# Batch norm on one core: the context closed after the first issues, parameter rows on ScalarE's queue, the first tile in one transfer

## The chip, the cores and the metric

The kernel runs on one core of a Trainium2 chip; the other cores are idle. The metric is the device time of one execution in microseconds, the median over the runs shown. Lower is better.

## The reference

The input `x` is float32 of shape (32, 256, 128, 128), 537 MB. Each of the 256 channels has its own gamma, beta, running mean and running variance:

```python
mean = running_mean.reshape(1, -1, 1, 1)
var = running_var.reshape(1, -1, 1, 1)
return gamma * (x - mean) / np.sqrt(var + 1e-5) + beta
```

For each channel this is one scale, gamma / sqrt(var + eps), and one shift, beta - mean * scale, applied to every element. All of `x` is read once and an output of the same size is written once.

## The kernel before

**Tiles.** A tile is 128 channels of one image: 128 partitions by 128 * 128 = 16384 float32, 8.39 MB. There are 32 * 2 = 64 of them (`NT`), taken in `order`: first all images' lower 128 channels, then the upper ones. Three buffers t0, t1, t2 (`NBUF`) hold tiles in SBUF; tile i lies in buffer i % 3 and is overwritten in place by its result.

**Engines.** SyncE issues the loads, on DMA queue q1. VectorE computes the first 14336 columns (`VCOLS`) of a tile in two instructions, 2560 (`STEP`) and 11776 wide (L162, L163, both through L133). ScalarE computes the last 2048 columns (L144) and issues the store (L157), on DMA queue q10. In the last tile VectorE does 9216 columns (`VLAST`) and ScalarE 7168.

**Order.** Everything stands in one `tc.tile_critical()` block with waits written by hand, so no scheduler orders it. `loaded[s]`, `stored[s]` count the transfers of a buffer (16 for each finished one), `vdone` VectorE's parts, `adone` ScalarE's.

- Load i, from the fourth on, waits until the store of tile i-3 has left its buffer and until VectorE has done the first part of tile i-1 (L104 to L107). So one load is in flight at a time.
- VectorE's first part of tile i waits until tile i has landed.
- ScalarE's part of tile i waits until VectorE has finished the tile and until the store of tile i-1 has landed (L165 to L169). So one store is in flight at a time.

**Parameters.** The four parameter vectors are loaded as rows: each is broadcast into 16 partitions of `rows`, 1 KB in each (L94). VectorE transposes 32x32 blocks (L111) and copies them (L116), so that a channel's values come to its partition. ScalarE takes the square root (L118); VectorE makes the reciprocal, the scale and the shift (L125 to L128). The helper `step` chains these on the semaphore `vec`.

**The beginning.** SyncE issues, in this order: the left half of tile 0 (L91, semaphore `early`), the four rows (L94, the first waits for the memset of `rows` at L92), the right half of tile 0 (L98), then tiles 1 and 2 whole (L105). VectorE does the left half of tile 0 when `early` and the parameters are there, the rest (6144 columns) when the right half has landed (L159, L160).

**The end.** SyncE waits for the last store of each buffer (L175). Then the tile context is closed: every engine goes through barriers, and GpSimd clears the context's semaphores. The buffers come from pools of the context, after a filler of 936 columns (`PAD`).

Of the kernel before, what the change touches and what calls it, by code (L numbers as in the profile page):

```python
# [8 lines left out]
NBUF = 3  # L9
PAD = 936  # L10


STEP = 2560
VCOLS = 14336
VLAST = 9216


@with_exitstack
def kernel(
    ctx: ExitStack,  # L20
    tc: tile.TileContext,
    x: bass.AP,
    gamma: bass.AP,
    beta: bass.AP,
    running_mean: bass.AP,
    running_var: bass.AP,
    out: bass.AP,
):
    nc = tc.nc
    eps = 1e-5  # L30
    f32 = mybir.dt.float32

    N, C, H, W = x.shape
    P = nc.NUM_PARTITIONS
    assert C % P == 0
    NCB = C // P
    HW = H * W
    NT = N * NCB
    B = 32
    NQ = P // B  # L40
    NE = 16
    NPAR = 4

    xr = x.rearrange("n (cb p) h w -> (n cb) p (h w)", p=P)
    outr = out.rearrange("n (cb p) h w -> (n cb) p (h w)", p=P)

    params = ctx.enter_context(tc.tile_pool(name="params", bufs=1))
    data = ctx.enter_context(tc.tile_pool(name="data", bufs=1))
    params.tile([P, PAD], f32, name="pad", tag="pad")
    bufs = [data.tile([P, HW], f32, name=f"t{s}", tag=f"t{s}") for s in range(NBUF)]  # L50
    rows = params.tile([B, NPAR * C], f32, name="rows", tag="rows")
    turned = params.tile([B, NPAR * C], f32, name="turned", tag="turned")
    par = params.tile([P, NPAR, NCB], f32, name="par", tag="par")
    eps_t = params.tile([P, 1], f32, name="eps_t", tag="eps")
    std_t = params.tile([P, NCB], f32, name="std_t", tag="std")
    rstd_t = params.tile([P, NCB], f32, name="rstd_t", tag="rstd")
    scale_t = params.tile([P, NCB], f32, name="scale_t", tag="scale")
    ms_t = params.tile([P, NCB], f32, name="ms_t", tag="ms")
    shift_t = params.tile([P, NCB], f32, name="shift_t", tag="shift")

    loaded = [tc.alloc_semaphore(f"loaded{s}") for s in range(NBUF)]
    stored = [tc.alloc_semaphore(f"stored{s}") for s in range(NBUF)]
    early = tc.alloc_semaphore("early")
    vdone = tc.alloc_semaphore("vdone")
    adone = tc.alloc_semaphore("adone")
    fetched = tc.alloc_semaphore("fetched")
    vec = tc.alloc_semaphore("vec")
    act = tc.alloc_semaphore("act")  # L70

    with tc.tile_critical():  # L72
        count = [0]

        def step(inst, sem=None, value=None):

            if sem is not None:
                inst._wait_ge(sem, value)
            elif count[0]:
                inst._wait_ge(vec, count[0])  # L80
            inst.then_inc(vec, 1)
            count[0] += 1
            return count[0]

        left, right = slice(0, HW // 2), slice(HW // 2, HW)
        last = NT - 1
        order = [n * NCB + cb for cb in range(NCB) for n in range(N)]

        nc.sync.dma_start(out=bufs[0][:, left], in_=xr[order[0]][:, left]).then_inc(early, 16)  # L91
        zeroed = step(nc.vector.memset(rows[:], 0.0))  # L92
        for r, ap in enumerate((running_var, gamma, beta, running_mean)):
            inst = nc.sync.dma_start(out=rows[0:NE, r * C : (r + 1) * C], in_=ap.partition_broadcast(NE))  # L94
            if r == 0:
                inst._wait_ge(vec, zeroed)
            inst.then_inc(fetched, 16)
        nc.sync.dma_start(out=bufs[0][:, right], in_=xr[order[0]][:, right]).then_inc(loaded[0], 16)  # L98
        for i in range(1, NT):
            s, turn = i % NBUF, i // NBUF  # L100


            if turn:
                nc.sync.wait_ge(stored[s], 16 * turn)  # L104
            inst = nc.sync.dma_start(out=bufs[s][:], in_=xr[order[i]]).then_inc(loaded[s], 16)  # L105
            if turn:
                inst._wait_ge(vdone, 2 * (i - 1) + 1)  # L107


        step(nc.vector.memset(eps_t[:], eps))  # L110
        step(nc.vector.transpose(out=turned[:], in_=rows[:]), fetched, 16 * NPAR)  # L111

        blocks = turned.rearrange("p (rc q b) -> p rc q b", q=NQ, b=B)
        flat = par.rearrange("p r cb -> p (r cb)")
        for q in range(NQ):
            placed = step(nc.vector.tensor_copy(out=flat[q * B : (q + 1) * B], in_=blocks[:, :, q, 0]))  # L116
        var_t, gamma_t, beta_t, mean_t = (par[:, r] for r in range(NPAR))
        nc.scalar.activation(  # L118
            out=std_t[:],
            in_=var_t,  # L120
            func=mybir.ActivationFunctionType.Sqrt,
            bias=eps_t[:],
            scale=1.0,
        )._wait_ge(vec, placed).then_inc(act, 1)
        step(nc.vector.reciprocal(out=rstd_t[:], in_=std_t[:]), act, 1)  # L125
        step(nc.vector.tensor_mul(out=scale_t[:], in0=gamma_t, in1=rstd_t[:]))  # L126
        step(nc.vector.tensor_mul(out=ms_t[:], in0=mean_t, in1=scale_t[:]))  # L127
        ready = step(nc.vector.tensor_sub(out=shift_t[:], in0=beta_t, in1=ms_t[:]))  # L128
        nc.vector.wait_ge(vec, ready)

        def vector_part(i, first, end):
            t, cb = bufs[i % NBUF], order[i] % NCB
            return nc.vector.tensor_scalar(  # L133
                out=t[:, first:end],
                in0=t[:, first:end],
                scalar1=scale_t[:, cb : cb + 1],
                scalar2=shift_t[:, cb : cb + 1],
                op0=mybir.AluOpType.mult,
                op1=mybir.AluOpType.add,
            ).then_inc(vdone, 1)  # L140

        def scalar_part(i, first):
            t, cb = bufs[i % NBUF], order[i] % NCB
            return nc.scalar.activation(  # L144
                out=t[:, first:],
                in_=t[:, first:],
                func=mybir.ActivationFunctionType.Identity,
                bias=shift_t[:, cb : cb + 1],
                scale=scale_t[:, cb : cb + 1],
            ).then_inc(adone, 1)  # L150

        def landed(i):
            return loaded[i % NBUF], 16 * (i // NBUF + 1)

        def store(i):
            s = i % NBUF
            nc.scalar.dma_start(out=outr[order[i]], in_=bufs[s][:])._wait_ge(adone, i + 1).then_inc(stored[s], 16)  # L157

        vector_part(0, 0, HW // 2)._wait_ge(early, 16)  # L159
        vector_part(0, HW // 2, VCOLS)._wait_ge(*landed(0))  # L160
        for i in range(1, NT):
            vector_part(i, 0, STEP)._wait_ge(*landed(i))  # L162
            vector_part(i, STEP, VLAST if i == last else VCOLS)  # L163
        for i in range(last):
            nc.scalar.wait_ge(vdone, 2 * (i + 1))  # L165
            inst = scalar_part(i, VCOLS)
            if i:
                inst._wait_ge(stored[(i - 1) % NBUF], 16 * ((i - 1) // NBUF + 1))
            store(i)  # L169
        scalar_part(last, VLAST)._wait_ge(*landed(last))  # L170
        nc.scalar.wait_ge(vdone, 2 * NT)
        store(last)

        for s in range(NBUF):
            nc.sync.wait_ge(stored[s], 16 * ((NT - s + NBUF - 1) // NBUF))  # L175


# [28 lines left out]
```

## Time and profile before

| | |
|---|---|
| runs | 2482.06, 2484.93 and 2484.79 us |
| median | 2484.79 us |
| span of the profiled execution (first to last instruction) | 2481.7 us |
| VectorE busy | 508.8 us |
| ScalarE busy | 140.0 us |
| bytes moved, mean rate over the span | 1073.85 MB, 433 GB/s |
| first load issued | 0.95 us after the first instruction |
| tile 0 landed (right half) | 23.61 us |
| first store issued | 29.27 us |
| first load that waits for a buffer (load 3) issued | 89.36 us |
| last store landed | 2480.4 us |

The page gives no time of the profiled execution other than its span. Idle time of an engine is listed with what ended it. The two largest items show what the compute engines wait for:

```profile
L133 DVE TENSOR_SCALAR t<-t,scale_t,shift_t 128x11776 f32<-128x11776 f32 (+2 forms) x128 | 505.3, 3989 | 1929.1 <-DMA t<-in_x_dram 1929.0
L144 ACT ACTIVATE t<-t,shift_t,scale_t 128x2048 f32<-128x2048 f32 x64 | 138.4, 2163 | 2297.8 <-DMA out_dram<-t 2275.0
```

The columns are: line, engine, operation, output and inputs, shape, count; busy us and mean ns of one; idle us of the engine just before them and what ended most of it. VectorE (DVE) waits for loads, ScalarE (ACT) for stores. The DMA queues are listed with packets, bytes and the time of their packets as a share of 16 engines' span:

```profile
q1 hardware_dynamic: 9488, 536.94, 50.1%
q10 hardware_dynamic: 9216, 536.88, 49.9%
```

q1 holds what SyncE issued, q10 what ScalarE issued. A tile is 128 data packets of 64 KB, one for each partition, and 16 packets of 4 bytes that count up its semaphore, one for each DMA engine. Behind the page lies a record for each packet with its queue, start, duration and size; where the text speaks of packet records, it means these.

### The profile page before, as it was taken

What the parts mean: (1) busy time and instruction counts of PE and PEld (TensorE: products, weight loads), DVE (VectorE), ACT (ScalarE), POOL (GpSimd) and SP (SyncE); (2) the same over time, 40 slices, a digit from 0 to 9 for tenths busy, and PEclk for the clock granted to TensorE, in tenths of its full rate; (3) what the DMA queues carried; (4) which work ended last, traced back from release to release, by engine and by line L of the source; (5) the groups of instructions that cost most, each with busy time, mean ns of one, the idle gap of its engine ahead of it and who ended that gap; (6) DMA issues with size and microseconds to landing.
All of it is one profiled execution on the core that took longest, in us unless ns stands there. A gap on an engine that the chain in (4) does not pass through costs nothing.

```text
span 2481.7 us, 516 instructions
## 1 busy us (share of the span) xinstructions
DVE 508.8 (21%) x139; ACT 140.0 (6%) x66; POOL 0.2 (0%) x4
## 2 busy tenths in 40 slices
DVE  2122121221212212122121221212212122121120
ACT  0000000000000000000000000000000000000001
POOL 0000000000000000000000000000000000000000
DMA  9999999999999999999999999999999999999999
GB/s 418 427 437 436 428 435 438 429 436 436 431 434 436 435 430 436 429 436 435 430 436 435 434 431 431 434 436 435 431 435 437 429 435 437 429 436 436 433 433 408
DMA packets 18708, 1073.85 MB, mean 433 GB/s; under 512 B 2128, under 2 KB 2192, under 8 KB 2192
## 3 DMA queue, kind: packets, MB, share of 16 engines
q1 hardware_dynamic: 9488, 536.94, 50.1%
q10 hardware_dynamic: 9216, 536.88, 49.9%
q14 instruction: 4, 0.03, 0.0%
HBM read 536.94 MB, written 536.87 MB: 433 GB/s over the span
## 4 chain that ended last, share of the span: by engine, by line
DMA 92%; DVE 4%; another core or an unknown queue 2%; ACT 0%; issue 0%; SPq 0%; DVEq 0%
DMA t<-in_x_dram 92%; DVE t L133 4%; ACT t L144 0%; SPq L94 0%; DVE rows L92 0%; DVE eps_t L110 0%; DVEq L201 0%; SPq L72 0%
## 5 line engine op out<-in xcount | busy, mean ns | idle before, releaser
L133 DVE TENSOR_SCALAR t<-t,scale_t,shift_t 128x11776 f32<-128x11776 f32 (+2 forms) x128 | 505.3, 3989 | 1929.1 <-DMA t<-in_x_dram 1929.0
L144 ACT ACTIVATE t<-t,shift_t,scale_t 128x2048 f32<-128x2048 f32 x64 | 138.4, 2163 | 2297.8 <-DMA out_dram<-t 2275.0
L111 DVE STREAM_TRANSPOSE turned<-rows 32x1024 f32<-32x1024 f32 x1 | 1.2, 1232 | 12.1 <-DMA rows<-in_running_mean_dram 12.1
L118 ACT ACT_TABLE_LOAD x1 | 1.3, 1283 | 0.9 <-SPq L72 0.9
L92 DVE MEMSET rows<- 32x1024 f32 x1 | 0.9, 912 | 1.2 <-SPq L72 1.2
L118 ACT ACTIVATE std_t<-par,eps_t 128x2 f32<-128x2 f32 x1 | 0.3, 297 | 14.3 <-DVE par L116 14.3
L116 DVE COPY par<-turned 32x8 f32<-32x8 f32 x4 | 0.6, 161 | 0.1
L125 DVE RECIPROCAL rstd_t<-std_t 128x2 f32<-128x2 f32 x1 | 0.2, 166 | 0.4 <-ACT std_t L118 0.4
L127 DVE TENSOR_TENSOR ms_t<-par,scale_t 128x2 f32<-128x2 f32 x1 | 0.2, 161 | 0.0
L128 DVE TENSOR_TENSOR shift_t<-par,ms_t 128x2 f32<-128x2 f32 x1 | 0.2, 161 | 0.0
L126 DVE TENSOR_TENSOR scale_t<-par,rstd_t 128x2 f32<-128x2 f32 x1 | 0.2, 160 | 0.0
L190 POOL MEMSET const-uint8-127<- 128x1 uint8 x1 | 0.1, 102 | 0.0
L190 POOL MEMSET const-bfloat16-1.0<- 128x1 bf16 x1 | 0.1, 101 | 0.0
L190 POOL MEMSET const-float32-0.0<- 128x1 f32 x1 | 0.1, 99 | 0.2 <-issue 0.2
L190 POOL MEMSET const-float32-1.0<- 128x1 f32 x1 | 0.1, 99 | 0.0
L110 DVE MEMSET eps_t<- 128x1 f32 x1 | 0.1, 59 | 0.1
## 6 DMA issues: line engine op xcount, KB each, us to landing
t<-in_x_dram SPq DMA_DIRECT2D x2, 4096.0 KB, 16.2
out_dram<-t ACTq DMA_DIRECT2D x64, 36.5
t<-in_x_dram SPq DMA_DIRECT2D x63, 37.0
rows<-in_running_var_dram SPq DMA_DIRECT2D x1, 16.0 KB, 11.3
rows<-in_gamma_dram SPq DMA_DIRECT2D x1, 16.0 KB, 11.2
rows<-in_beta_dram SPq DMA_DIRECT2D x1, 16.0 KB, 11.0
rows<-in_running_mean_dram SPq DMA_DIRECT2D x1, 16.0 KB, 10.9
```

Of the source, the lines that this page charges most:

```text
L92: zeroed = step(nc.vector.memset(rows[:], 0.0))
L110: step(nc.vector.memset(eps_t[:], eps))
L111: step(nc.vector.transpose(out=turned[:], in_=rows[:]), fetched, 16 * NPAR)
L116: placed = step(nc.vector.tensor_copy(out=flat[q * B : (q + 1) * B], in_=blocks[:, :, q, 0]))
L118: nc.scalar.activation(out=std_t[:], in_=var_t, func=mybir.ActivationFunctionType.Sqrt, bias=eps_t[:], scale=1.0,)._wait_ge(vec, placed).t ...
L125: step(nc.vector.reciprocal(out=rstd_t[:], in_=std_t[:]), act, 1)
L126: step(nc.vector.tensor_mul(out=scale_t[:], in0=gamma_t, in1=rstd_t[:]))
L127: step(nc.vector.tensor_mul(out=ms_t[:], in0=mean_t, in1=scale_t[:]))
L128: ready = step(nc.vector.tensor_sub(out=shift_t[:], in0=beta_t, in1=ms_t[:]))
L133: return nc.vector.tensor_scalar(out=t[:, first:end], in0=t[:, first:end], scalar1=scale_t[:, cb : cb + 1], scalar2=shift_t[:, cb : cb + 1 ...
L144: return nc.scalar.activation(out=t[:, first:], in_=t[:, first:], func=mybir.ActivationFunctionType.Identity, bias=shift_t[:, cb : cb + 1] ...
L190: nc = _bacc.Bacc("TRN2", target_bir_lowering=False, num_devices=1)
```

## The change

1. The tile context is closed early. Only the memset of `rows`, the loads of tiles 0, 1 and 2 and the four row transfers stay inside; then come `tc.close()` and `tc.compile()`, and all that follows is issued plainly behind the context's closing barriers. The waits by hand are the same. Buffers and semaphores no longer come from the context, and SyncE clears the semaphores itself after the last store.
2. The four row transfers are issued by ScalarE in place of SyncE, and so go on queue q10.
3. Tile 0 is loaded in one transfer of 16384 columns. The semaphore `early` is gone, and VectorE treats tile 0 as every other tile: 2560 and 11776 columns after the whole has landed.

The filler and the sizes of the buffers stay. The core of the diff:

```diff
-    params = ctx.enter_context(tc.tile_pool(name="params", bufs=1))
-    data = ctx.enter_context(tc.tile_pool(name="data", bufs=1))
-    params.tile([P, PAD], f32, name="pad", tag="pad")
-    bufs = [data.tile([P, HW], f32, name=f"t{s}", tag=f"t{s}") for s in range(NBUF)]
+    def tile_of(name, *shape):
+        return nc.alloc_sbuf_tensor(name, list(shape), f32)
...
+    tile_of("pad", P, PAD)
+    bufs = [tile_of(f"t{s}", P, HW) for s in range(NBUF)]
...
+    sems = {name: nc.alloc_semaphore(name) for name in names}
...
     with tc.tile_critical():
-        nc.sync.dma_start(out=bufs[0][:, left], in_=xr[order[0]][:, left]).then_inc(early, 16)
+        nc.sync.dma_start(out=bufs[0][:], in_=xr[order[0]]).then_inc(loaded[0], 16)
         zeroed = step(nc.vector.memset(rows[:], 0.0))
         for r, ap in enumerate((running_var, gamma, beta, running_mean)):
-            inst = nc.sync.dma_start(out=rows[0:NE, r * C : (r + 1) * C], in_=ap.partition_broadcast(NE))
+            inst = nc.scalar.dma_start(out=rows[0:NE, r * C : (r + 1) * C], in_=ap.partition_broadcast(NE))
             if r == 0:
                 inst._wait_ge(vec, zeroed)
             inst.then_inc(fetched, 16)
-        nc.sync.dma_start(out=bufs[0][:, right], in_=xr[order[0]][:, right]).then_inc(loaded[0], 16)
-        for i in range(1, NT):
-            s, turn = i % NBUF, i // NBUF
+        for i in range(1, NBUF):
+            nc.sync.dma_start(out=bufs[i][:], in_=xr[order[i]]).then_inc(loaded[i], 16)
+    tc.close()
+    tc.compile()
 
-            if turn:
-                nc.sync.wait_ge(stored[s], 16 * turn)
-            inst = nc.sync.dma_start(out=bufs[s][:], in_=xr[order[i]]).then_inc(loaded[s], 16)
-            if turn:
-                inst._wait_ge(vdone, 2 * (i - 1) + 1)
+    for i in range(NBUF, NT):
+        s, turn = i % NBUF, i // NBUF
+        nc.sync.wait_ge(stored[s], 16 * turn)
+        inst = nc.sync.dma_start(out=bufs[s][:], in_=xr[order[i]]).then_inc(loaded[s], 16)
+        inst._wait_ge(vdone, 2 * (i - 1) + 1)
...
-        vector_part(0, 0, HW // 2)._wait_ge(early, 16)
-        vector_part(0, HW // 2, VCOLS)._wait_ge(*landed(0))
-        for i in range(1, NT):
-            vector_part(i, 0, STEP)._wait_ge(*landed(i))
-            vector_part(i, STEP, VLAST if i == last else VCOLS)
+    for i in range(NT):
+        vector_part(i, 0, STEP)._wait_ge(*landed(i))
+        vector_part(i, STEP, VLAST if i == last else VCOLS)
...
-        for s in range(NBUF):
-            nc.sync.wait_ge(stored[s], 16 * ((NT - s + NBUF - 1) // NBUF))
+    for s in range(NBUF):
+        nc.sync.wait_ge(stored[s], 16 * ((NT - s + NBUF - 1) // NBUF))
+    nc.sync.sem_clear(used)
```

## The prediction

> **What bounds the kernel now.** I read the page's head and DMA row first, then the chain of waits, the first 60 us of the timeline, then the DMA queues in short windows.
>
> ```profile
> span 2481.7 us, 516 instructions
> DVE 508.8 (21%) x139; ACT 140.0 (6%) x66; POOL 0.2 (0%) x4
> DMA  9999999999999999999999999999999999999999
> ```
>
> The DMA engines are full in all 40 slices and the compute engines are nearly idle. In the steady state two transfers are in flight, one load (queue q1, issued by SyncE) and one store (q10, issued by ScalarE). The chain of waits has the load side, the timeline the store side:
>
> ```profile
> 89.36 37.74 DMA t<-in_x_dram
> 127.12 1.62 DVE t L133
> 128.76 36.96 DMA t<-in_x_dram
> ```
>
> ```profile
> 72.37 2.10 ACT L144 ACTIVATE t<-t,shift_t,scale_t 128x2048 f32<-128x2048 f32 x1 [43.13 <-DMA out_dram<-t]
> 74.50 0.34 ACTq L157 DMA_DIRECT2D out_dram<-t  x1
> ```
>
> So load i+1 is issued 1.67 us after load i lands (VectorE's 2560 columns between them), and store k+1 2.15 us after store k lands (ScalarE's part). Each queue therefore runs empty for some us once a tile, and the other must have packets left to fill that hole. It does now: from load issue to load issue it takes 38.64 us (128.76 to 167.39). A tile is 128 packets of 65,536 bytes each way, 8 + 8 for each of the 16 engines, so a packet takes 38.64/16 = 2.415 us and nothing is lost. Whether the holes stay covered depends on how the two queues stand to each other, and that is set in the first 90 us, the stretch that the change rewrites.
>
> How the queues share is seen in the DMA queues of single packet times. From 51.9 to 54.3 us:
>
> ```profile
> q10 hardware_dynamic: 16, 1.05, 100.8%
> q1 hardware_dynamic: 15, 0.00, 0.4%
> ```
>
> q1's 15 packets carry nothing: they are tile 1's 4-byte semaphore packets. Tile 2's data stood right behind them in q1, and still each engine went back to q10 for a whole 65,536-byte packet. A 4-byte packet uses up a full turn. From 68.8 to 78.4, after store 0's last data packets:
>
> ```profile
> q1 hardware_dynamic: 64, 4.19, 101.7%
> q10 hardware_dynamic: 16, 0.00, 0.1%
> ```
>
> Four load packets per engine go by (9.66 us) before store 1 comes in: the hole of a store. The semaphore packet waited out one of them.
>
> **The change, part by part.** The sum is made against the profiled execution: its span of 2481.7 us. No other time of it is shown; the median of the runs, 2484.79, is 3.1 above, which I add at the end.
>
> *The end.* SyncE sees the last store at 2480.4; from there to 2481.7 are the barriers and the clearing of the closed context, 1.25 us.
>
> ```profile
> L72 SPq COMPARE_BRANCH  x1: 33/33/33, 2480.4 to 2480.4; - x1
> L201 POOLq EVENT_SEMAPHORE_RANGE_CLEAR  x1: 118/118/118, 2481.3 to 2481.3; - x1
> ```
>
> After the change one clear follows the wait: 0.12 us and its issue. Gain 1.0 us (bounds 0 and 1.25).
>
> *The barriers at the front.* The same 1.25 us now come after ScalarE's fourth row transfer, at about 4 to 5.3 us. Behind them stand VectorE's eps memset (0.06) and transpose, ScalarE's table load (1.28, no longer at 0.90) and SyncE's load 3. Cost 0: the first two engines wait for the rows anyway (below), and load 3 is not due before 80 us. Without that cover it would be 2.5 us, once. SyncE is spared four issues (0.34 to 0.44 each) between loads; its queue had 4 MB in stock then, so nothing is gained.
>
> *The rows on q10, the whole tile on q1.* Now, rows and first tile share one queue:
>
> ```profile
> 2.16 0.34 SPq L94 DMA_DIRECT2D rows<-in_running_var_dram  x1
> 14.40 1.23 DVE L111 STREAM_TRANSPOSE turned<-rows 32x1024 f32<-32x1024 f32 x1 [12.15 <-DMA rows<-in_running_mean_dram]
> 17.65 4.55 DVE L133 TENSOR_SCALAR t<-t,scale_t,shift_t 128x8192 f32<-128x8192 f32 x1
> 23.63 3.48 DVE L133 TENSOR_SCALAR t<-t,scale_t,shift_t 128x6144 f32<-128x6144 f32 x1 [1.44 <-DMA t<-in_x_dram]
> 27.15 2.10 ACT L144 ACTIVATE t<-t,shift_t,scale_t 128x2048 f32<-128x2048 f32 x1 [10.40 <-DVE t L133]
> 29.27 0.38 ACTq L157 DMA_DIRECT2D out_dram<-t  x1
> ```
>
> The rows lay behind half a tile; parameters took 17.65 - 14.38 = 3.27 us from their landing, and half of tile 0 was done before its other half came. Afterwards the rows are issued from 2.16 on another queue. The page counts 2192 - 2128 = 64 packets of 1 KB for 4 transfers, so every engine has 4 data and 4 semaphore packets: 8 turns, each alternating with a load packet of 2.415. No row shows 1 KB packets alternating; I price them like the 4-byte ones. The earliest start is behind the first packet of tile 0, so the last one comes as tile 0's eighth ends, with tile 0's own semaphore. That is 1.97 (first packet, in the packet records) + 8 x 2.415 + about 0.7 (opening and spread of engines) + 0.37 (from the semaphore packet to the landing, 71.98 to 72.35) = 22.4 to 23.4; I take 23.2 for both. Lower bound, if small packets got through at once: 8 to 10 us.
>
> Then 3.27 to the parameters (26.5), VectorE's two parts 7.94 (as tile 1's, 55.29 to 63.23) to 34.4, ScalarE 2.1: store 0 is issued at 36.6 in place of 29.27. The lost overlap is no loss in itself, since q1 has packets till about 60.
>
> *What is late next.* In the packet records tile 1's packets begin at 22.6 and store 0's at 35.1 on 15 of 16 engines (33.1 on one): 5 packets of tile 1 went ahead. After the change tile 1 begins near 22.3, its eighth packet runs from 39.2 to 41.6; a store issued at 36.6 comes in at the first boundary after 40.4 (3.8 later, as the early engine): 41.6. So 8 go ahead. From there store 0's 8 packets alternate with tile 2's; tile 1's semaphore takes one load turn, so 6 of tile 2 are used when the store's last packet ends. 2 are left, against 5 in the kernel before (the four above and one behind store 1's first).
>
> Those 2 fill 4.83 us of the store's hole. The hole from the store's last packet: one packet before the semaphore's turn 2.42, landing 0.37, ScalarE and issue 2.15, and from issue to packets. That last was 1.02 for the very first load (0.95 to 1.97), 1.86 with the slow opening of its first packets counted over 16 engines. It comes to 6.0 to 6.8, and 0.3 to 1.2 more since the slowest engine's semaphore counts. Both queues are empty for 1.1 us at least and 3.2 at most; I take 2.6, near the upper end, since the opening row is an idle engine as here.
>
> *It repeats.* Load 3's semaphore is 4.83 after the store's last packet, then 0.37 + 1.67 + 1.02: 7.9. Store 1's first packet starts at 6.4 to 7.4, its second at 8.8 or later, so the load joins behind the second. Then S S L S L ... S L, and again two load packets are left at the store's end. Some 61 rounds (loads 3 to 63) lose 2.6 each: 159 us.
>
> Sum: 2481.7 - 1.0 + 159 = 2639.7; with 3.1, 2643 us. A round would read 41.2 us for 38.6.
>
> [...]
>
> **Rivals.**
> 1. *The rows get through at once.* For it: no row shows 1 KB packets against a load. Against: the 4-byte ones. Tile 0 then sets the pace: 23.2 + 7.94 + 2.15 = 33.3, boundary after 37.1, six to seven packets of tile 1 ahead; with six the load packets last just until store 1 comes, no hole. Time: 2481.7 - 1.0 + 3.1 = 2484. Chance 0.09.
> 2. *The holes open and close again* (the other side, not slower). If load 3 comes in behind store 1's third packet, three load packets are left at the next store's end, 7.25 us, which covers the hole; the old order is back. It decides at 8.8 to 9.8 against my 7.9: one more us from issue to packets. For it: at 92.9 to 95.3 two of 16 engines missed their turn at load 3. Against: 1.02 in an idle queue. Price two rounds: 2484 + 5 = 2489. Chance 0.09.
> 3. *Lockstep.* If the load is back before the store's first packet, both end together and each round loses 0.37 + 1.67 + 1.86 = 3.9: 61 x 3.9 = 238, so 2722. It needs the load 0.5 to 1.5 earlier, or a store slower to start from idle. Chance 0.12.
>
> **How the numbers follow.** My forecast has 0.68, with its own range from 61 x 1.1 to 61 x 3.2 lost: 2551 to 2679. Faster by over 0.2% (5 us, about what these runs, 2482.06 to 2484.93, can tell from none) has no room: 1024 packets of 2.415 are 2473 of the 2481.7. 0.02. Within 0.2%: rivals 1 and 2, 0.17 (a heal just over 5 us left out). Slower: 0.81. The range must reach the unchanged cases and lockstep: 2481 to 2730.
>
> **What would show it.** Rows landing at 23 and not before 10; store 0 issued at 36 to 37; after 80 us a round of about 41 us in the chain, with a steady rate near 407 GB/s for 434 and a DMA row no longer full; load landings following store landings by about 2.4 us. I am wrong if store 0 is issued by 34, or if rounds of 38.6 return after the first few; the turn-by-turn price of small packets fails in the one case, the lasting order in the other.

## The result and the profile after

The changed kernel takes 2595.8 us in the median of four runs (2591.54 to 2603.5), the kernel before 2484.86 in four: a ratio of 1.0457, 95% interval 1.0445 to 1.0469. It is slower by about 111 us. The profiled execution took 2597.08 us with a span of 2595.8.

The head of the page after, with the DMA row:

```profile
span 2595.8 us, 515 instructions
DVE 508.7 (20%) x139; ACT 139.8 (5%) x66; POOL 0.2 (0%) x4
DMA  9999999999999999999999999999999999999999
```

The engines do the same work, and the DMA row is as full as before. The row hides the loss. The window from 300 to 2300 us shows it; the last two columns are the DMA engines' share and GB/s. First the kernel before, then the kernel after:

```profile
300.00:2300.00 2000.00, 412.63 (x104) 109.01 (x52) 0.00 (x0) 1.00 1.00 434
```

```profile
300.00:2300.00 2000.00, 388.82 (x98) 102.53 (x49) 0.00 (x0) 1.00 0.99 414
```

In 2000 us VectorE does 98 parts in place of 104, and the rate is 414 for 434 GB/s at nearly the same busy share. The chain of waits after, from 287 us (start, us, what):

```profile
287.79 40.50 DMA t<-in_x_dram
328.32 1.62 DVE t L127
329.96 37.73 DMA t<-in_x_dram
367.71 1.62 DVE t L127
369.35 37.75 DMA t<-in_x_dram
407.13 1.62 DVE t L127
408.77 40.38 DMA t<-in_x_dram
```

From load issue to load issue it is 42.2, 39.4, 39.4 us, where the kernel before has 38.66 in the mean (38.61 to 39.08). From load 3 (87.55) to load 63 (2517.77) the mean is 2430.2 / 60 = 40.50. Against the 38.64 of a full round that is 1.86 lost; 61 rounds x 1.86 = 113.5 us, and the span grew by 114.1. The loss is spread over all rounds; what set it is in the first 40 us. The rows' transfers in the page's list of DMA issues (last column: us from issue to landing) and the timeline:

```profile
rows<-in_running_var_dram ACTq DMA_DIRECT2D x1, 16.0 KB, 9.0
rows<-in_gamma_dram ACTq DMA_DIRECT2D x1, 16.0 KB, 14.1
rows<-in_beta_dram ACTq DMA_DIRECT2D x1, 16.0 KB, 19.0
rows<-in_running_mean_dram ACTq DMA_DIRECT2D x1, 16.0 KB, 21.5
```

```profile
3.53 0.44 ACTq L89 DMA_DIRECT2D rows<-in_running_mean_dram  x1
25.08 1.23 DVE L105 STREAM_TRANSPOSE turned<-rows 32x1024 f32<-32x1024 f32 x1 [20.01 <-DMA rows<-in_running_mean_dram]
28.32 7.93 DVE L127 TENSOR_SCALAR t<-t,scale_t,shift_t 128x2560 f32<-128x2560 f32 x2
36.29 2.09 ACT L138 ACTIVATE t<-t,shift_t,scale_t 128x2048 f32<-128x2048 f32 x1 [8.87 <-DVE t L127]
38.41 0.38 ACTq L151 DMA_DIRECT2D out_dram<-t  x1
```

From issue and landing, the rows land at 11.2, 16.7, 22.1 and 25.0: two load packets apart, but for the last, whose semaphore packet came right behind tile 0's. Store 0 is issued at 38.41 in place of 29.27. The two turns of the first row are seen in the DMA queues from 7.3 to 9.8 us:

```profile
q1 hardware_dynamic: 16, 1.05, 96.7%
q10 hardware_dynamic: 16, 0.02, 1.8%
```

That is one 1 KB packet and one 65,536-byte packet for each of 16 engines. From 9.8 to 12.2 it is the same with the 4-byte semaphore packets. A 1 KB packet takes a turn of its own, as priced. What the late store 0 leaves is seen in the DMA queues from 77.0 to 84.25 us, behind store 0's last data packets:

```profile
q1 hardware_dynamic: 48, 3.15, 100.1%
q10 hardware_dynamic: 16, 0.00, 0.1%
```

Three load packets per engine go by before store 1 comes in, and they are tile 2's last; in the kernel before it was four, with more behind them.

The end went as the change means it. One clear follows the last store's landing at 2595.72:

```profile
L168 SPq EVENT_SEMAPHORE_RANGE_CLEAR  x1: 45/45/45, 2595.7 to 2595.7; - x1
```

From the last landing to the end it is 0.06 us, against 1.27 (2480.42 to 2481.69).

### The profile page after: what moved, and what is told of

The parts are those of the page before. It is cut to its first block, busy times and chain, and to the rows that moved or that the text cites. A ratio compares the mean times of both kernels' runs of the same rounds, so it can differ in the third digit from the quotient of the medians.

```text
span 2595.8 us, 515 instructions
## 1 busy us (share of the span) xinstructions
DVE 508.7 (20%) x139; ACT 139.8 (5%) x66; POOL 0.2 (0%) x4
## 4 chain that ended last, share of the span: by engine, by line
DMA 92%; DVE 5%; another core or an unknown queue 2%; ACT 0%; issue 0%; ACTq 0%; DVEq 0%; SPq 0%
DMA t<-in_x_dram 91%; DVE t L127 4%; DMA rows<-in_running_mean_dram 1%; ACT t L138 0%; ACTq L89 0%; DVE turned L105 0%; DVE rows L87 0%; DVE par L110 0%; ACT std_t L112 0%; DVE rstd_t L119 0%; DVE shift_t L122 0%; DVE scale_t L120 0%; DVE ms_t L121 0%; DVEq L96 0%
## 5 line engine op out<-in xcount | busy, mean ns | idle before, releaser
L127 DVE TENSOR_SCALAR t<-t,scale_t,shift_t 128x2560 f32<-128x2560 f32 (+1 forms) x128 | 505.2, 3989 | 2028.3 <-DMA t<-in_x_dram 2028.2
## 6 DMA issues: line engine op xcount, KB each, us to landing
rows<-in_running_mean_dram ACTq DMA_DIRECT2D x1, 16.0 KB, 21.5
```

The lines of the kernel that those rows point to most:

```text
L127: return nc.vector.tensor_scalar(out=t[:, first:end], in0=t[:, first:end], scalar1=scale_t[:, cb : cb + 1], scalar2=shift_t[:, cb : cb + 1 ...
```

## The experiments

The theory: what store 0's issue time sets is how the load queue and the store queue stand to each other; that order is kept for all 61 rounds, and in the bad one a hole of a queue is not covered. A time without a count of runs is one execution; the kernel before, timed beside them, took 2481.89 to 2485.71 us. "Packets ahead" below are tile 1's data packets that each DMA engine started before its first packet of store 0, from the packet records; a round is the mean from load 6 to load 63.

### One part at a time

**The closed context alone.** The changed kernel with the head of the kernel before:

```diff
-        nc.sync.dma_start(out=bufs[0][:], in_=xr[order[0]]).then_inc(loaded[0], 16)
+        left, right = slice(0, HW // 2), slice(HW // 2, HW)
+        nc.sync.dma_start(out=bufs[0][:, left], in_=xr[order[0]][:, left]).then_inc(early, 16)
...
-            inst = nc.scalar.dma_start(out=rows[0:NE, r * C : (r + 1) * C], in_=ap.partition_broadcast(NE))
+            inst = nc.sync.dma_start(out=rows[0:NE, r * C : (r + 1) * C], in_=ap.partition_broadcast(NE))
...
+        nc.sync.dma_start(out=bufs[0][:, right], in_=xr[order[0]][:, right]).then_inc(loaded[0], 16)
...
-    for i in range(NT):
+    vector_part(0, 0, HW // 2)._wait_ge(early, 16)
+    vector_part(0, HW // 2, VCOLS)._wait_ge(*landed(0))
+    for i in range(1, NT):
```

> The changed kernel with the head of the kernel before: tile 0 in two halves and the rows on SyncE's queue between them; the context still closes behind the first issues. Theory (the order of the two queues, set by when store 0 is issued): store 0 is issued near 29.3 us as before, five packets of tile 1 go ahead of it, rounds of 38.64 us, span about 2480.5, that is the kernel before less the 1.2 us of closing barriers. Rival (buffers and semaphores outside the context, or its barriers at the front, slow the stream): rounds of 40.5 us and about 2595.

Store 0 was issued at 28.98, five packets ahead (four on three engines), rounds of 38.67. The median is 2481.0 us in 11 runs against 2482.43 in 15; ratio 0.9994, interval 0.9985 to 1.0003. The 1.2 us are seen in the trace (last landing 2479.36, end 2479.42) and are too few for the times to tell. Addresses, semaphores and front barriers cost nothing that shows.

**The rows alone.** The kernel before with

```diff
-            inst = nc.sync.dma_start(out=rows[0:NE, r * C : (r + 1) * C], in_=ap.partition_broadcast(NE))
+            inst = nc.scalar.dma_start(out=rows[0:NE, r * C : (r + 1) * C], in_=ap.partition_broadcast(NE))
```

> The kernel before with the four row transfers issued by ScalarE, nothing else changed. Theory: the rows land at about 25 us as in the changed kernel (eight small packets, each behind a load packet), the parameters come at 28.3; the halves are then both there, so VectorE takes 8.0 us and ScalarE 2.1 more: store 0 at 38.4, rounds of 40.5, about 2596. Rival (the whole first tile is the cause, the rows are not): store 0 stays below 34 and the time is 2485.

A miss: 2484.86 us, rounds of 38.67. The rows landed at 16.6, not 25. The DMA issues of this run:

```profile
rows<-in_running_var_dram ACTq DMA_DIRECT2D x1, 16.0 KB, 7.2
rows<-in_gamma_dram ACTq DMA_DIRECT2D x1, 16.0 KB, 9.5
rows<-in_beta_dram ACTq DMA_DIRECT2D x1, 16.0 KB, 11.0
rows<-in_running_mean_dram ACTq DMA_DIRECT2D x1, 16.0 KB, 13.0
```

I had carried the 25 us over from the changed kernel. But with halves, tile 0's packets are 32,768 bytes and took 1.36 us here in the median, so a turn beside them costs little more than half of one beside a 65,536-byte packet of 2.42 us. Parameters came at 19.8, the left half was done while the right was still coming, and store 0 went out at 30.76 behind four packets.

**The whole tile alone.** The kernel before with tile 0 in one transfer and the rows behind it on SyncE's queue:

```diff
-        nc.sync.dma_start(out=bufs[0][:, left], in_=xr[order[0]][:, left]).then_inc(early, 16)
+        nc.sync.dma_start(out=bufs[0][:], in_=xr[order[0]]).then_inc(loaded[0], 16)
...
-        nc.sync.dma_start(out=bufs[0][:, right], in_=xr[order[0]][:, right]).then_inc(loaded[0], 16)
...
-        vector_part(0, 0, HW // 2)._wait_ge(early, 16)
-        vector_part(0, HW // 2, VCOLS)._wait_ge(*landed(0))
-        for i in range(1, NT):
+        for i in range(NT):
```

> The kernel before with tile 0 loaded in one transfer, the rows behind it on SyncE's queue. Theory: rows and tile 0 land at about 22.8 to 23.2, parameters at 26.3, store 0 at 36.4, first served at the boundary near 41.6 after eight packets of tile 1: the holes open, rounds near 40.5, about 2595. Rival (only the rows' way through ScalarE's queue does it): 2485.

2592.88 us: store 0 at 37.63, eight packets ahead, rounds of 40.43. As expected; this part alone brings the loss.

**The whole tile with the parameters at hand.** The changed kernel with the rows issued by SyncE ahead of tile 0:

```diff
-        nc.sync.dma_start(out=bufs[0][:], in_=xr[order[0]]).then_inc(loaded[0], 16)
         zeroed = step(nc.vector.memset(rows[:], 0.0))
...
-            inst = nc.scalar.dma_start(out=rows[0:NE, r * C : (r + 1) * C], in_=ap.partition_broadcast(NE))
+            inst = nc.sync.dma_start(out=rows[0:NE, r * C : (r + 1) * C], in_=ap.partition_broadcast(NE))
...
-        for i in range(1, NBUF):
+        for i in range(NBUF):
```

> The changed kernel with the rows issued by SyncE ahead of tile 0, which stays one transfer; tile 0 then starts 2.5 to 3 us later. Theory: parameters are there by 10 us, so store 0 follows tile 0's landing by 7.94 + 2.15 = 10.1 us in place of 13.5. Counted from tile 0's landing that lies between the run with two spare activations (6.6 us, 2484) and the changed kernel (13.6, 2597), and just over the run with five (9.9, 2592): so about 2595, one transfer is too late even with the parameters at hand. Rival (the rows alone make the changed kernel slow): 2488.

2592.92 us. The parameters were there at 9.6; store 0 still came 10.12 us after tile 0's landing (36.05 after 25.93), behind six packets on 13 engines and seven on three. Rounds of 40.45. The missing half-tile overlap is enough by itself.

### The order of the queues by itself

**One later load, once.** The changed kernel; only load 3 waits for both parts of tile 2:

```diff
-        inst._wait_ge(vdone, 2 * (i - 1) + 1)
+        inst._wait_ge(vdone, 2 * (i - 1) + (2 if i == NBUF else 1))
```

> The changed kernel with one wait made longer, once: load 3 waits until VectorE has done both parts of tile 2 and not only the first, so it is issued 6.3 us later, at about 94. Theory: meanwhile only store 1 runs, which covers it; the load comes in some three packets of the store later, five or more load packets are left when the store ends, every later hole is covered, rounds of 38.64 from then on: about 2488 in place of 2597, so a later issue gains 110 us. Rival (the rounds are long for another reason: addresses, code, the closed context): 2597 or more, by the 6.3 us.

2486.26 us. The chain of waits of this run:

```profile
81.82 7.95 DVE t L127 x2
89.78 39.09 DMA t<-in_x_dram
128.90 1.62 DVE t L127
130.53 37.30 DMA t<-in_x_dram
```

Load 3 goes out 8 us after tile 2's landing in place of 1.67. The first rounds behind it still take 39.0 to 40.8; from load 6 on the mean is 38.69, with rows, whole tile and closed context all as in the slow kernel and eight packets ahead. The rate is 434 GB/s again. So addresses, code, rows, whole tile and closed context do not make the rounds long by themselves. In several executions:

> The changed kernel with load 3 alone issued one VectorE part later, timed in several executions. Theory: the order that load 3 sets holds in each of them, 2484 to 2490, the same as the kernel before at 2%. Rival (the first look caught a lucky execution, and the order falls either way): some executions near 2597.

The median is 2484.9 us in 10 runs (2484.61 to 2486.86), against 2482.69 in 13 of the kernel before: ratio 1.001, interval 1.0 to 1.0019. The profiled one has rounds of 38.66. No execution fell into the long rounds.

**A later store 0 in the kernel before.** Here nothing of the change is made; ScalarE does n spare activations before it issues store 0:

```diff
             if i:
                 inst._wait_ge(stored[(i - 1) % NBUF], 16 * ((i - 1) // NBUF + 1))
+            if i == 0:
+                for j in range(8):
+                    inst = nc.scalar.activation(out=rows[:], in_=turned[:], func=mybir.ActivationFunctionType.Identity)
+                    inst._wait_ge(act, 1 + j).then_inc(act, 1)
             store(i)
```

Eight:

> The kernel before, in which ScalarE does eight spare activations of 32x1024 (about 1.1 us each, one behind the other) once, between its part of tile 0 and store 0; the results are used by nobody. Everything else, rows, halves, context, stays. Theory: store 0 is issued near 38.5 us, where the changed kernel has it (38.41), eight packets of tile 1 go ahead, the holes open for good: about 2596, over 110 us for 9 us of spare work. Rival (a late first store costs what it is late, or is hidden under the loads): 2485 to 2494.

Two:

> The same with two spare activations: store 0 near 31.6 us, first served behind six packets of tile 1 in place of five. Theory: six load packets ahead still leave four for the store's hole (9.66 us): rounds of 38.64, 2485. Rival (any delay of store 0 costs in proportion): a quarter of what eight cost, about 2513 if those cost 111.

Five:

> The same with five: store 0 near 35 us, first served behind seven packets of tile 1. Three load packets, 7.25 us, are left for a hole of 6.6 to 7.5: the theory cannot say which side it falls on, but says that it is one or the other, near 2486 or near 2596, since each order of the queues restores itself. Rival (cost in proportion to the delay): about 2555.

Three, to part five from six and seven:

> The kernel before with three spare activations ahead of store 0 (two put it at 30.11 us and behind five packets of tile 1, five at 33.28 and behind six on 14 engines and seven on two). Store 0 should be issued near 31.2 and come in behind six on all engines. Theory as written in the prediction: with six ahead four load packets are left for the store's hole, all of it is covered: 2485. Rival (six is too many already; then the two engines with seven did not decide the run with five): about 2592.

| spare | store 0 issued, us | packets ahead | round, us | time, us |
|---|---|---|---|---|
| none | 29.27 | 5 (four on one engine) | 38.66 | 2484.86 (median) |
| 2 | 30.11 | 5 | 38.71 | 2484.46 |
| 3 | 31.15 | 5 on nine engines, 6 on seven | 38.68 | 2484.58 |
| 5 | 33.28 | 6 on fourteen, 7 on two | 40.41 | 2591.55 |
| 8 | 36.58 | 8 | 40.47 | 2595.48 |

In these runs there are two outcomes and nothing between: 2.1 us more of delay, from three to five, cost 107 us, the 3.3 us from five to eight cost 4. The first two spare activations put store 0 only 0.84 us later, each further one 1.04 to 1.10. With three, they ran from 28.99 to 32.20 us and store 0 went out at 31.15, before their end. So the runs with two and three did not reach the counts expected. Whether six on all engines still covers the hole, as the prediction had it, was not reached: six on seven engines do, six on fourteen with seven on two do not.

The packet records say more. A store has landed when its last engine is done, and only then is the next one issued. With five spare activations store 0's semaphore packets came at 73.7 to 74.2 on fourteen engines and at 76.9 on the two with seven ahead, and the landing was at 77.24. With three, the engines with six ahead came last (74.1 to 75.1), and the landing was at 75.45. So the largest count is the one to read: in the runs that change only what stands before store 0 it is four to six where the rounds stay short and seven or eight where they are long. That fits the prediction, though it is read off afterwards.

### What a round loses

**A shorter way from store to store.** The changed kernel with

```diff
-VCOLS = 14336
+VCOLS = 15872
```

> The changed kernel with ScalarE's part cut from 2048 to 512 columns and VectorE's widened to 15872 in all tiles but the last. ScalarE's part falls from 2.1 to about 0.85 us, and with it the time from a store's landing to the next store's issue. Theory: what a round loses is the part of the store's hole that the load packets don't cover, so rounds fall from 40.5 by up to 1.25, to 39.3 (not under 38.64): about 2520. Rival (the load's side or the DMA engines themselves set the 40.5): 2597 unchanged.

2550.44 us, rounds of 39.84: the direction of the theory, but a gain of 47 us where 77 were expected. The trace shows another order. A store is now issued 0.87 us after the landing of the one before, a load still 1.67, and the order drifts: store k lands 33.8 us after load k+1 at k = 1, then 30.1, 24.1, 19.8, 14.4 and further, until it is near 4.8 or 9.6 in almost every round. Now the load's hole is the one with too few packets of the other queue: 18% of q1's data packets between 300 and 2300 us took over 2.5 us, and none of q10's, where in the changed kernel it was 8% and 13%. Whether the good order needs turns of like length besides a good start was not shown; no run started this kernel in the good order.

**A longer way from load to load.** The changed kernel with

```diff
-STEP = 2560
+STEP = 5120
```

> The changed kernel with VectorE's first part of each tile 5120 columns wide in place of 2560, so that every load is issued about 1.6 us later after the landing of the one before (3.3 for 1.67 us). Theory (second rival of the prediction, made to happen): the load comes in at least one store packet later, one more load packet is left for the store's hole, and the order moves back to covered holes within some rounds: about 2490. Rival (a longer way from load to load makes each round longer): 2597 + 62 x 1.6, about 2696.

Neither came: 2545.63 us, rounds of 39.68. The load is issued 3.00 us after the landing in place of 1.67. The chain of waits:

```profile
1115.54 2.96 DVE t L127
1118.51 35.99 DMA t<-in_x_dram
1154.53 2.96 DVE t L127
1157.51 37.06 DMA t<-in_x_dram
```

The order does not go back, but each round loses 1.04 in place of 1.86. In this run every load from load 3 on landed 4.8 to 5.6 us after the store before it, which at 2.42 us a packet means that three load packets were left for the store's hole; the rounds with only two, which the changed kernel has (below), do not occur. So a longer wait on the critical chain gained 50 us. That three left do not bring back 38.64 is what the expectation had wrong.

## Why the prediction was right, and where it was off

**The mechanism held.** Rows turn by turn, a late store 0, holes of a queue left uncovered, and the order lasting to the end: each stands in the trace after (rows landed at 11.2 to 25.0, store 0 issued at 38.41, no data packet started between 1136.6 and 1138.9, rounds of 40.50 in the mean from load 3 to load 63), and the later load 3 undoes the long rounds without touching any other part (38.69). Delaying store 0 alone brings them about in the kernel before (40.41 and 40.47).

**The head, term by term.** Rows at 23.2 predicted, 25.0 measured; store 0 at 36.6, measured 38.41. The number of turns was right, but 65,536-byte packets took 2.5 to 2.9 us between 12.2 and 20.7 us and 2.8 to 2.9 between 23 and 43, for 2.42 (packet records). So tile 1 came later and slower: seven packets went ahead, not eight, and three load packets per engine ran between store 0's last and store 1's first, not two. Why the packets were slow stays open. The rows' packets can't be all of it, since the rows had landed at 25.0. Four other profiles have the same head (load 3 later, twice; the shorter and the longer way): the rows landed at 24.0 to 25.8 and store 0 was issued at 37.34 to 38.66, with eight ahead in three and seven in one. The direction did not hang on this: the loss came with store 0 at 33.28 already.

**The loss of a round was mis-sized:** 2.6 predicted, 1.86 measured; 61 rounds made 113.5 us for 159. The step that failed is that two load packets are left in every round. On the DMA engine that ends the store last, a load that lands 2.4 us behind the store had two left, one that lands 4.8 us behind it three, since the store's own semaphore packet waits out one: at the store that landed at 283.73 one engine's semaphore packet came at 283.36, the other 15 at 280.2 to 281.0. Of 56 rounds 38 began with three left (a store landed at 121.12, the load at 125.95) and took 39.8 us in the mean; 15 began with two (283.73 and 286.13) and took 42.2; three fit neither. So a round with two lost 3.6, more than the 2.6, and one with three, which the prediction counted as covered, lost 1.2. The two errors offset each other in part: that 1.86 lies inside the bounds of 1.1 and 3.2 is partly luck.

**The hole does not look as I said.** "A DMA row no longer full" was wrong. Between 300 and 2300 us, engines without a data packet make 0.43 us a round; the rest, about 1.4, lies in packets that were recorded longer: 13% of q10's data packets took over 2.5 us (0.02% before), 8% of q1's (1.5%). Most of them are among the first 16 packets of a transfer, which took 2.95 us in the mean for stores and 2.93 for loads, against 2.42 and 2.43 before. They count as busy. Why they are slow stays open.

**Which part does it.** The prediction laid the late store to the rows and the whole tile together, and called the lost overlap of the halves "no loss in itself". The runs put it on the overlap: without it store 0 is too late even with the parameters at 9.6 us. ScalarE's queue for the rows is harmless beside halves (2484.86 us). Beside a whole tile no added delay shows: store 0 went out at 37.63 with the rows on SyncE's queue, at 37.34 to 38.66 in the five profiles with them on ScalarE's. The closing of the context gives 1.2 us (1.0 predicted).

**The added 3.1 us** for what lies around the span was too much. Where both figures are known, an execution of the kernel before takes about 1.8 us beyond its span (2481.91 and 2480.1), and the changed kernel 1.3 (2597.08 and 2595.8); the rest was a difference between executions.

**The rivals.** The first fell with the rows' landings. Its price was also doubtful: it had store 0 at 33.3, and the run with store 0 at 33.28 took 2591.55 us, not 2484. So a store 0 issued by 34 would not by itself have meant short rounds. The second, holes that close again, did not come by itself: its condition, three load packets left, was there in most rounds and did not bring the old order back. Load 3 made later by 6.3 us did, 1.3 us on every load did not. Lockstep was not seen: the means of rounds stay at 40.5, under 42.5.

## What to carry to other kernels

In this kernel a load stream and a store stream share saturated DMA engines (a share of 0.99 to 1.00) and each waits for its own landing. Each then has a hole once a tile (a load is issued 1.67 us after the landing of the one before, a store 2.15), and the other must have packets left to fill it; how they stood to each other was set in the first 90 us and lasted to the end. In a kernel of this kind, read a change at the front by when the first store goes out against the loads, not by what it hides behind. Where rounds are longer than their bytes explain, try shifting one transfer by some microseconds, once; here 6.3 us on load 3 brought the rounds from 40.50 to 38.69.

## What the runs showed of the hardware

- The DMA engines took one packet from each queue in turn in the windows shown, of 2.4 and 2.5 us: from 7.3 to 9.8 in the changed kernel 16 packets of 1 KB went by with 16 of 65,536 bytes, from 9.8 to 12.2 16 of 4 bytes with 16, from 51.9 to 54.3 in the kernel before 15 of 4 bytes with 16. So a small transfer was priced by the other queue's packets: the last of four rows took 21.5 us to land beside 65,536-byte packets and 13.0 where the first ones were of 32,768.
- The DMA share stayed at 0.99 (1.00 before) with 5% less moved; the rate (414 for 434 GB/s), the rounds and the lengths of packets told it.
- In the kernel before, 2.1 us more delay of one store cost 107 us (2484.58 to 2591.55); in the changed kernel, 6.3 us of delay of one load gained 111 (2597.08 to 2486.26).
